# One store of a matmul kernel in 18 transfers: seven m tiles, 752 columns of the eighth, and its last 16 columns by 15, 14, down to 1, and 8 partitions

## Chip, cores and metric

One core of a Trainium2 chip. The metric is the device time of one execution in microseconds; a profile is one execution taken by the hardware profiler, and its span is shorter than that execution's time (208.6 and 210.41 for the kernel before). Runs were on several chips, so each kernel's time is compared with runs of the kernel before on the same chip. A profile of the kernel before was taken once, on the first chip; where a profile of an experiment is set against it, the chips can differ.

## The reference

```python
batch, m, k, n = 16, 512, 1024, 768
def reference(x, weight, sub_value):          # all float32
    return (np.matmul(x, weight) - sub_value).astype(np.float32)
```

Flattened, that is 8192 rows (64 m tiles of 128) by 1024 by 768; 87 MB go through the DMA engines: 62 MB read, 25 MB written.

## The kernel before

All transfers are issued from SyncE in the order of one list, `(kind, first m tile, number of m tiles)`. A transfer that is not ready holds up those after it (in the profile of before, SyncE stands still for up to 26.5 us before one of them).

```python
TRANSFERS = [
    ...                                             # loads of x ('x'), weight ('w') and sub_value ('s')
    ('o', 24, 8), ('o', 32, 8), ('s', 56, 8), ('o', 40, 8), ('o', 48, 8), ('o', 56, 5),
    ('o', 61, 2), ('o', 63, 1),                     # 'o': store
]
```

A store of eight tiles takes 24576 contiguous bytes from each of 128 partitions. Each issue waits for what it needs and adds 16 to a semaphore when it has landed:

```python
            if kind == "o":
                waits.append((counter["finish"], max(finish_at[t] for t in need)))
                ...
            sem, value = lane((kind, at))
            ...
            if kind == "o":
                here, there = there, here
            sp.add(lambda here=here, there=there: nc.sync.dma_start(out=here, in_=there), waits, (sem, 16))
```

sub_value and the result share one ring of 32 m tiles (`so_ring`): DVE subtracts in place. The tiles 40 to 47 are not loaded over again, so nothing waits for their store but the end of the kernel.

## Time and profile before

| | before |
|---|---|
| time, median of 2 | 210.31 us (210.26 to 210.35) |
| span of the profile | 208.6 us |
| last subtraction ends | 202.64 us |
| last store issued | 202.66 us |
| its first engine lands / its last engine lands | 204.86 / 207.29 us |
| SyncE instructions recorded | 68 |

The landings are read from the records of semaphore increments: each of the 38 transfers of the kernel before has 16 of them, 608 in all, one for each DMA engine that has finished its share, and the trace has the time of each. The prediction below shows the profile's lines and how they are read.

### The profile page before, as it was taken

The numbers are of one execution on the slowest core, as the hardware profiler recorded it, in microseconds if no ns is written. First come the engines' busy times: TensorE is split into PE (matmuls) and PEld (weight loads), VectorE is DVE, ScalarE is ACT, GpSimd is POOL, SyncE is SP. The second block draws the span as 40 slices with busy tenths as digits, with TensorE's granted clock in tenths as the row PEclk, the third lists the DMA queues.
The fourth block names the chain that finished last, engine by engine and source line by source line (L and its number), as shares of the span: only waits on it lengthen the run. The fifth ranks groups of instructions, "written<-read, shape, count | busy, mean of one in ns | idle before, by whom it ended". The sixth has DMA issues, their size and how long they took to land.

```text
span 208.6 us, 2612 instructions
## 1 busy us (share of the span) xinstructions
PE 195.2 (94%) x1234; PEld 75.5 (36%) x700; DVE 128.2 (61%) x224; ACT 109.0 (52%) x113; POOL 1.0 (0%) x7
## 2 busy tenths in 40 slices
PE   6999799969999999999999999999999999999960
PEld 0233243324434433443443443343344344334410
DVE  2323224975993795598399379469739938952330
ACT  3655759506673761944745576183564737507300
POOL 1000000000000000000000000000000000000000
PEclk9999999999999999999999999999999999999997
DMA  6999999999999999999999999999999999999993
GB/s 204 421 427 434 441 424 434 445 429 424 434 448 452 366 443 424 459 415 418 449 440 424 419 429 443 423 470 393 434 463 401 441 424 429 438 443 419 419 422 135
DMA packets 5476, 87.08 MB, mean 417 GB/s; under 512 B 608, under 2 KB 608, under 8 KB 1888
## 3 DMA queue, kind: packets, MB, share of 16 engines
q1 hardware_dynamic: 5472, 87.03, 97.9%
q8 instruction: 1, 0.02, 0.0%
q14 instruction: 3, 0.02, 0.0%
HBM read 61.87 MB, written 25.17 MB: 417 GB/s over the span
## 4 chain that ended last, share of the span: by engine, by line
PE 75%; DMA 13%; DVE 6%; SPq 3%; issue 1%; DVEq 0%
PE po_b L198 67%; DMA so_ring<-in_sub_value_dram 13%; PE pt_b L335 8%; DVE xtp_b L368 3%; DVE so_ring L417 2%; SPq L298 2%; SPq L262 1%; SPq L553 0%; DVEq L59 0%; SPq L138 0%
## 5 line engine op out<-in xcount | busy, mean ns | idle before, releaser
L198 PE MATMUL po_b<-w_sb,xt_b 128*128 128x384 f16 x704 | 126.0, 326 | 1.2 <-DVE w_sb L265 0.9
L417 DVE TENSOR_TENSOR so_ring<-po_b,so_ring 128x768 f32<-128x768 f32 x64 | 60.8, 957 | 59.3 <-PE po_b L198 39.9
L348 ACT COPY xt_b<-pt_b 128x1024 f16<-128x1024 f16 x44 | 44.5, 1012 | 65.3 <-PE pt_b L335 64.3
L368 DVE STREAM_TRANSPOSE xtp_b<-x16p_b 32x256 f32<-32x256 f32 x144 | 62.7, 435 | 2.3
L198 PE MATMUL po_b<-w_sb,xtp_b 128*128 128x384 f16 x320 | 61.3, 326 | 1.9 <-DVE xtp_b L368 1.7
L397 PEld LDWEIGHTS <-xt_b 128*128 128x128 f16 x352 | 34.4, 98 | 58.9 <-issue 55.6
L317 ACT CAST x_b<-x_ring 128x1024 f16<-128x1024 f32 x46 | 47.2, 1048 | 5.0 <-DMA x_ring<-in_x_dram 4.9
L335 PE MATMUL pt_b<-ident,x_b 128*128 128x128 f32 x184 | 47.5, 274 | 1.7 <-ACT x_b L317 1.7
L335 PEld LDWEIGHTS pt_b<-ident,x_b 128*128 128x128 f32 x184 | 25.4, 141 | 44.6 <-issue 36.8
L317 ACT CAST x16p_b<-x_ring 128x1024 f16<-128x1024 f32 x18 | 18.8, 1046 | 14.9 <-DMA x_ring<-in_x_dram 14.9
L397 PEld LDWEIGHTS <-xtp_b 128*128 128x128 f16 x160 | 15.7, 98 | 20.4 <-issue 18.3
L265 DVE CAST w_sb<-so_ring 128x768 f16<-128x768 f32 x8 | 4.1, 556 | 11.6 <-DMA so_ring<-in_weight_dram 11.6
L198 PE MATMUL po_b<-idle_x,idle_w 128*128 128x512 f16 x26 | 7.7, 448 | 1.7 <-POOL idle_x L178 1.7
L348 ACT COPY xtp_b<-pt_b 128x1024 f16<-128x1024 f16 x2 | 2.0, 1012 | 2.5 <-PE pt_b L335 2.5
L317 ACT ACT_TABLE_LOAD x1 | 1.3, 1283 | 0.9 <-SPq L138 0.9
L427 PEld LDWEIGHTS <-idle_w 128*128 128x128 f16 x4 | 0.4, 99 | 1.7 <-POOL idle_x L178 1.7
L187 DVE TENSOR_TENSOR ident<-along,across 32x32 f32<-32x32 f32 x4 | 0.7, 183 | 0.1
L179 DVE MEMSET ones<- 128x32 f32 x1 | 0.1, 85 | 1.0 <-SPq L138 1.0
L178 POOL MEMSET idle_x<- 128x512 f16 x1 | 0.5, 528 | 0.0
L499 ACT CAST stub<-ident 128x1 f16<-128x1 f32 x2 | 0.4, 194 | 0.0
L184 DVE STREAM_TRANSPOSE across<-along 128x32 f32<-128x32 f32 x1 | 0.2, 212 | 0.0
L476 POOL MEMSET mark<- 128x1 f32 x1 | 0.1, 98 | 23.7 <-ACT xtp_b L348 23.7
(7 smaller groups left out, 1.0 us busy)
## 6 DMA issues: line engine op xcount, KB each, us to landing
so_ring<-in_sub_value_dram SPq DMA_DIRECT2D x7, 3072.0 KB, 24.2
out_dram<-so_ring SPq DMA_DIRECT2D x7, 3072.0 KB, 26.6
x_ring<-in_x_dram SPq DMA_DIRECT2D x5, 4096.0 KB, 23.1
x_ring<-in_x_dram SPq DMA_DIRECT2D x2, 2048.0 KB, 27.2
so_ring<-in_weight_dram SPq DMA_DIRECT2D x4, 768.0 KB, 8.3
x_ring<-in_x_dram SPq DMA_DIRECT2D x1, 3072.0 KB, 28.8
x_ring<-in_x_dram SPq DMA_DIRECT2D x2, 1024.0 KB, 24.8
out_dram<-so_ring SPq DMA_DIRECT2D x1, 1920.0 KB, 10.2
```

Of the source, the lines that this page charges most:

```text
L178: pool.add(lambda: nc.gpsimd.memset(idle_x, 0.0), then=count("idle"))
L187: dve.add(lambda here=here: nc.vector.tensor_tensor(out=ident[here, here], in0=along[here], in1=across[here], op=mybir.AluOpType.is_equal, ...
L198: return nc.tensor.add_instruction(mybir.InstMatmult(name=nc.get_next_instruction_name(), engine=full.engine, ins=list(full.ins), outs=lis ...
L262: sp.add(lambda st=st, at=at: nc.sync.dma_start(out=st, in_=w_c[at]), then=(sem, 16))
L265: lambda at=at, r=r, st=st: nc.vector.tensor_copy(out=w_sb[:, at, r], in_=st[:, r]),
L298: sp.add(lambda here=here, there=there: nc.sync.dma_start(out=here, in_=there), waits, (sem, 16))
L317: act.add(lambda: nc.scalar.copy(out=to, in_=x_in), waits, count("cast"))
L335: pe.add(lambda: nc.tensor.transpose(words, from_, ident), waits, count("turn") if last else None)
L348: act.add(lambda: nc.scalar.copy(out=to, in_=pt_b[:, b]), waits, count("evac"))
L368: dve.add(lambda: nc.vector.transpose(xt[b * Q : (b + 1) * Q, :, a * Q : (a + 1) * Q], x16[a * Q : (a + 1) * Q, :, b * Q : (b + 1) * Q],), ...
L397: pe.add(lambda weights=weights: nc.tensor.ldweights(weights, tile_position=(0, 0)), [w for w in waits if w[0] in ready])
L417: dve.add(lambda: nc.vector.tensor_tensor(out=o, in0=po[:, :, :NS], in1=o, op=mybir.AluOpType.subtract), [landed["s", mi], (counter["mul"] ...
```

## The change

What the pattern is for, the code does not say; it names it `MARKED` and `PARTS`. The prediction assumes that a transfer of p partitions uses p DMA engines, and the same ones first each time, so that each of the first 15 small transfers uses one engine fewer than the one before it. The packet records have no engine numbers: engine 0, 1, ... are names, by the number of small transfers that an engine carries. The pattern either marks the engines in a trace or delays them by that number. The result of the kernel is the same.

```diff
+MARKED, PARTS = 40, tuple(range(15, 0, -1)) + (8,)
...
-            sp.add(lambda here=here, there=there: nc.sync.dma_start(out=here, in_=there), waits, (sem, 16))
+            if (kind, at) != ("o", MARKED):
+                sp.add(lambda here=here, there=there: nc.sync.dma_start(out=here, in_=there), waits, (sem, 16))
+                continue
+            edge, low = 752, 0
+            sp.add(lambda here=here, there=there: nc.sync.dma_start(out=here[:, : n - 1], in_=there[:, : n - 1]), waits, (sem, 16))
+            one = lane((kind, at, "edge"))
+            lanes_of = next(l for l in lanes if l["sem"] is one[0])
+            lanes_of["value"] += 16 * len(PARTS)
+            sp.add(lambda here=here, there=there: nc.sync.dma_start(
+                out=here[:, n - 1 :, :edge], in_=there[:, n - 1 :, :edge]
+            ), then=(one[0], 16))
+            for part in PARTS:
+                high = low + part
+                sp.add(lambda low=low, high=high, here=here, there=there: nc.sync.dma_start(
+                    out=here[low:high, n - 1 :, edge:], in_=there[low:high, n - 1 :, edge:]
+                ), then=(one[0], 16))
+                low = high
+            assert low == P
```

## The prediction

> **What bounds the kernel now.** I read the page's parts 1 and 2 first, then the table of windows, the chain of waits, the issues of the SyncE queue in order of time, and last the raw records behind them: one record per DMA packet (start, duration, size, but no engine number) and one per semaphore increment by a DMA.
>
> ```profile
> PE 195.2 (94%) x1234; PEld 75.5 (36%) x700; DVE 128.2 (61%) x224; ACT 109.0 (52%) x113; POOL 1.0 (0%) x7
> PE   6999799969999999999999999999999999999960
> ...
> DMA  6999999999999999999999999999999999999993
> GB/s 204 421 427 434 441 424 434 445 429 424 434 448 452 366 443 424 459 415 418 449 440 424 419 429 443 423 470 393 434 463 401 441 424 429 438 443 419 419 422 135
> ...
> q1 hardware_dynamic: 5472, 87.03, 97.9%
> ```
>
> Two things are full at once: TensorE (94%), and the 16 DMA engines (97.9% of the span, nine tenths or more in every slice but the first and the last). Which of them sets the end must be read at the end. The table of windows (columns: stretch, its length, busy us of each engine, granted clock, DMA share, GB/s):
>
> ```profile
> 180.00:190.00 10.00, 10.00 (x66) 3.79 (x36) 5.66 (x9) 4.23 (x7) 0.00 (x0) 1.00 1.00 430
> 190.00:200.00 10.00, 10.00 (x66) 3.94 (x37) 3.79 (x4) 3.98 (x4) 0.00 (x0) 1.00 1.00 430
> 200.00:204.00 4.00, 1.64 (x11) 0.39 (x4) 0.99 (x2) 0.00 (x0) 0.00 (x0) 1.00 0.95 402
> 204.00:206.00 2.00, 0.00 (x0) 0.00 (x0) 0.00 (x0) 0.00 (x0) 0.00 (x0) 1.00 0.54 220
> 206.00:208.60 2.60, 0.00 (x0) 0.00 (x0) 0.00 (x0) 0.00 (x0) 0.00 (x0) 0.51 0.04 15
> ```
>
> TensorE stops at 201.64, the last subtraction ends at 201.68 + 0.96 = 202.64, and the last store is issued at 202.66. The DMA engines are still full then, and run out one by one after 204: share 0.54, then 0.04. In the packet records every engine works without a gap up to its last packet; none waits for the last store. So the last stretch is bound by DMA bytes already queued, and the end is set by the engine that is furthest behind. The increments of the last store's semaphore show how far: the first engine lands at 204.86, twelve of them by 205.49, then 206.09, 206.48, 206.96 and 207.29. I call this last engine A: it is 2.43 us behind the first. The lags grew early: after landings with a spread of 0.7 us up to 28.7, A jumps to 1.80 at the landing of 32.3 and to 2.45 at 71.5, and then stays (2.43 at 112.7, 2.43 at 190.2). Between those jumps the engines keep the same pace. The runner-up is 0.3 us ahead of A.
>
> The chain of waits puts 75% on PE and 13% on the load of sub_value. Because it goes back from the last store through the last subtraction, it hides this DMA backlog; I don't read the bound of the last stretch from it.
>
> The stores concerned, from the timeline of the SyncE queue (start, duration):
>
> ```profile
> 170.88 0.34 SPq L298 DMA_DIRECT2D so_ring<-in_sub_value_dram  x1
> 171.27 0.62 SPq L298 DMA_DIRECT2D out_dram<-so_ring  x1
> ...
> 181.17 0.33 SPq L298 DMA_DIRECT2D out_dram<-so_ring  x1
> ...
> 194.32 0.33 SPq L298 DMA_DIRECT2D out_dram<-so_ring  x1
> ...
> 200.06 0.33 SPq L298 DMA_DIRECT2D out_dram<-so_ring  x1
> ```
>
> The store at 171.27 is the one that is split (m tiles 40 to 47). By its semaphore it lands at 190.24 to 192.67, since a store and the last sub_value load are queued before it. The next issue, at 181.17, waits for the subtraction of m tile 55.
>
> [...]The kernel before only has 128-partition transfers[...]: 38 transfers, 608 four-byte packets, 16 each. [...]the next data packet starts 4 to 6 ns after a semaphore packet does, though the increment is seen some 0.33 us later (206.96 and 207.29 for A).[...]
>
> **The change, part by part.** Bytes, waits, computing and the rest of the queue stay; 17 issues are added on SyncE. The order comparison shows the same rows on PE, DVE, ACT and POOL and 63 rows against 45 on SP (some rows merge repeats).
>
> (1) *SyncE's time.* One more issue costs 0.43 us (median of the ten stores). From 171.27: 0.62 + 17 x 0.48 (0.43 and the 0.05 gap seen between issues) = 8.8, so done at about 180.1. The next issue comes at 181.17. Free, with 1.1 us to spare; and even if an issue on fewer engines takes 0.7 us, the late store is at 184, while the engines have work queued up to about 190. Cost 0.
>
> (2) *The split of the rows into seven tiles and 752 columns.* Each engine gets 8 packets of 21504 B and 8 of 3008 B in place of 8 of 24576 B, and one semaphore packet more. Packets of 3072 B follow each other by about 117.5 ns, of 15360 B by about 569 ns: 36.7 ps per byte, and 4.6 ns for a packet. So 8 x 4.6 + 6 (semaphore packet) = 0.04 us on every engine.
>
> (3) *The 16 small ones.* [...]Engine 0 gets 16 of them (15 and the last 8), engine 7 gets 8 + 1 = 9, engine 8 gets 7, engine 14 one, engine 15 none; 128 in all, 8 on average. By the fit of (2), a small one is 64 x 0.0367 + 4.6 + 6 = 13 ns; with the recorded durations (8 ns for the 40-byte packets, 9 ns for a semaphore packet) it is about 19. [...]Engine 0: 16 x 19 = 0.30 us, at 60 ns 1.0 us. An average engine: 0.15 us, or 0.5.
>
> (4) *What of it counts.* All of this lies inside the backlog, and no buffer waits for this store (no sub_value load comes after the one at 170.88). What A gets is paid in full at the end. An engine ahead of A pays only what exceeds its lead: 12 of 16 engines lead by at least 1.8 us and can't become last below 110 ns for a small one. The numbers of A and the runner-up aren't in the records. If A is engine 15: +0.04. If it is engine 0: +0.34, up to +1.1 us. On average over the places, +0.2 at 19 ns, +0.5 at 60. I take +0.3 us.
>
> Sum: 210.31 + 0.3 = 210.6 us. The intent looks like moving a little work by engine number, or marking the engines: transfers that each leave out one engine more. But it takes no work off a late engine: 64 B of 8 rows are 512 B, 0.02 us.
>
> **The rivals.** (R1) *A small semaphore write stalls its engine.* If 16 stalls of 0.33 us come in a row, engine 0 is 5.3 us late; minus its lead, the end comes 3 to 5 us later, 213.3 to 215.6. Against it: 4 to 6 ns after every semaphore packet before. For it: they were never nearer together than 0.94 us per engine. 6%. (R2) *The number of transfers that may be outstanding is limited.* At the start, the 14th, 15th and 16th issue take 0.98, 1.65 and 2.13 us instead of 0.43. About 10 transfers, or about 90 packets per engine, were outstanding then. If packets are the limit: at the end of the small issues engine 0 has about 24 + 9 + 32 = 65, no block. If transfers are: SyncE blocks after some six small ones until the queue drains at 185 to 192, the next store is issued late, at about 193 to 196, and the engines run dry for 2 to 5 us: 212.5 to 215.5. 10%. (R3) *An instruction fetch falls elsewhere.* Four packets of 8 or 16 KB of other queues lie in the span (at 30.9, 50.4, 87.5, 146.0), and after each of them one engine's lag jumps by 0.5 to 1.1 us. SyncE's stream grows from 68 to 85 instructions; should that bring one more fetch or another engine, the end moves by up to 1 us either way. 10%. (R4) *A gain*: only by R3, or if the end is not set by A; under 0.3 us.
>
> **Range and chances.** The plain sum gives 210.35 to 210.65, dear small writes up to 211.4; R3 adds up to 1 us; R1 and R2 make the upper tail. The two runs of before differ by 0.09. Prediction 210.6, eight times in ten within 210.2 to 211.8. Two per cent are 4.2 us: slower needs R1 or R2 in full, 5%; faster has no source, 1%.
>
> **What would show each step.** (1) 55 issues on SyncE; the small ones at some 0.48 us each; the next store still at about 181.2. An issue of over 1 us, or a later store, speaks for R2. (2) and (3): 128 packets of 64 B at about 10 ns; small transfers landing with k increments by DMA, 15 down to 1 and 8; the time between the landings of the split store and the next one, 7.27 us before, grows by 0.04 us on the engine without small ones and by up to 0.3 on the one with 16. A gap of 0.3 us after each small one is R1. (4) The last store's landing at 207.3 to 207.7, TensorE and DVE unchanged. The prediction is wrong if the DMA share falls below 0.9 between 185 and 200, or if the spread of the last landing exceeds 3.5 us.

## The result, and the profile after

212.69 us (212.67 to 212.70, 2 runs) against 210.31: ratio 1.0109, 95% interval 1.0085 to 1.0133. A ratio here is the mean time of one kernel's fast runs over that of the other's fast runs of the same rounds, so it is not quite the ratio of the medians quoted; the differences in us given for the experiments are these ratios times the time before. The kernel is 2.4 us slower, and outside the range of 210.2 to 211.8.

The page of the changed kernel (parts 1 to 3):

```profile
PE 195.7 (93%) x1234; PEld 75.5 (36%) x700; DVE 128.1 (61%) x224; ACT 108.9 (52%) x113; POOL 1.0 (0%) x7
...
DMA  5999999999999999999999999999999999999991
GB/s 197 421 427 432 435 423 443 444 427 430 424 462 429 390 443 424 416 466 395 438 466 404 443 438 406 472 416 407 477 416 420 448 420 415 422 414 395 407 398 68
DMA packets 5877, 87.08 MB, mean 413 GB/s; under 512 B 880, under 2 KB 880, under 8 KB 2288
```

The engines do the same work. The packets below 512 B went from 608 to 880: 128 small ones and 144 semaphore packets (16 for the 752 columns, 128 for the small transfers). The table of windows of the changed kernel, and of the one before for the first two stretches:

```profile
190.00:192.00 2.00, 2.00 (x16) 0.95 (x9) 0.96 (x1) 1.47 (x2) 0.00 (x0) 1.00 1.27 400
192.00:194.00 2.00, 2.00 (x15) 0.90 (x9) 0.59 (x1) 0.92 (x2) 0.00 (x0) 1.00 0.95 363
...
200.00:204.00 4.00, 1.71 (x11) 0.39 (x4) 1.07 (x2) 0.00 (x0) 0.00 (x0) 1.00 0.94 402
204.00:206.00 2.00, 0.00 (x0) 0.00 (x0) 0.00 (x0) 0.00 (x0) 0.00 (x0) 1.00 0.77 316
206.00:208.00 2.00, 0.00 (x0) 0.00 (x0) 0.00 (x0) 0.00 (x0) 0.00 (x0) 0.73 0.28 115
208.00:211.00 3.00, 0.00 (x0) 0.00 (x0) 0.00 (x0) 0.00 (x0) 0.00 (x0) 0.50 0.03 11
```

```profile
190.00:192.00 2.00, 2.00 (x15) 0.94 (x9) 0.96 (x1) 1.54 (x2) 0.00 (x0) 1.00 1.03 442
192.00:194.00 2.00, 2.00 (x15) 0.91 (x8) 0.67 (x1) 0.92 (x2) 0.00 (x0) 1.00 1.11 479
```

This is the main reading. TensorE is as busy as before, and works until 201.71 (before: 201.64). Between 190 and 194, where the small transfers are worked off, the DMA engines stay busy by the share, but carry 400 and 363 GB/s instead of 442 and 479: over 4 us, 2 x (442 + 479 - 400 - 363) = 316 KB less. The engines are occupied without moving bytes. (A share over 1 is possible because packets are counted by the time at which they start.)

SyncE's queue issued the small ones without trouble:

```profile
171.26 0.70 SPq L304 DMA_DIRECT2D out_dram<-so_ring  x1
172.00 0.71 SPq L308 DMA_DIRECT2D out_dram<-so_ring  x1
172.76 7.44 SPq L313 DMA_DIRECT2D out_dram<-so_ring  x16
181.24 21.82 SPq L301 DMA_DIRECT2D out_dram<-so_ring  x4
```

Sixteen issues in 7.44 us, and the next store at 181.24 against 181.17. The time was lost on the DMA engines. The packet records (times in ns from the span's start) of one engine, whose small ones can be told apart because the engine is late:

```
start   end     took  bytes
192488  192497     9      4     semaphore packet of the 752 columns
192494  192505    11     64     1st small one; 13 small ones and 13 semaphore packets, 13 ns from one to the next
...
192657  192666     9      4     13th semaphore packet
192662  194422  1760  24576     next store: 912 ns otherwise
194419  195919  1500  24576
```

The small ones are passed in 13 x 13 = 169 ns, as predicted. The two packets behind them take 1760 and 1500 ns instead of 912: 1.44 us more. The number of small ones in a row names the engine, if the same engines come first in every transfer: 13 small ones is engine 3, the only one that is then in the 12 transfers of 15 down to 4 and in the last of 8. The extra time of the packets behind, for the engines told with certainty: 2 or 3 small ones 0; 5 (engine 10) 0; 6 (engine 9) 0.18; 12 (engine 4) 1.63; 13 (engine 3) 1.44; 15 (engine 1) 1.65 us. The other engines, told apart by the distance between two packets, fit between: 7 about 0.34, 9 to 11 about 1.0 to 1.4, 16 (engine 0) 1.92. In sum 12.2 us over 16 engines, 0.76 each; at 430 GB/s that is 328 KB, the 316 KB missing in the windows.

The increments of the last store's semaphore give the end: first engine 205.20 (before 204.86), last engine 209.09 (before 207.29). In the change, engine 3 is last. It was 2.38 us behind the first engine when the seven tiles landed, 0.17 us of small packets and 1.44 us of stretching make 3.99; measured 3.89. Engine 10, which was last before the small ones, 3.03 us behind the first, had only five of them and is passed.

After the last landing there are 1.8 us to the end of the span, against 1.3 before. The profile's view of the last lines of SyncE, before and after (columns: operation, duration min/median/max in ns, first and last start in us):

```profile
L526 SPq EVENT_SEMAPHORE  x1: 17/17/17, 207.5 to 207.5; - x1
L526 SPq DRAIN  x1: 7/7/7, 207.6 to 207.6; - x1
```

```profile
L545 SPq EVENT_SEMAPHORE  x1: 17/17/17, 209.3 to 209.3; - x1
L545 SPq DRAIN  x1: 124/124/124, 209.7 to 209.7; - x1
```

The gap between the two instructions was 68 ns and is 430 ns, and the drain itself takes 124 instead of 7: 0.48 us, with nothing waited for that the profile shows.

So the spans' difference of 2.3 us is 1.8 us of later landing and 0.5 us behind it. Of the 1.8, some 0.16 is not the change's: the load of x tiles 56 to 63 already begins to land at 161.29 instead of 161.13, before anything is different.

### The profile page after: what moved, and what is told of

It is laid out like the page before. It is cut to its first block, busy times and chain, and to the rows that moved or that the text cites.

```text
span 210.9 us, 2630 instructions
## 1 busy us (share of the span) xinstructions
PE 195.7 (93%) x1234; PEld 75.5 (36%) x700; DVE 128.1 (61%) x224; ACT 108.9 (52%) x113; POOL 1.0 (0%) x7
## 4 chain that ended last, share of the span: by engine, by line
PE 74%; DMA 13%; DVE 5%; SPq 3%; issue 1%; DVEq 0%
PE po_b L200 67%; DMA so_ring<-in_sub_value_dram 13%; PE pt_b L354 7%; DVE xtp_b L387 3%; DVE so_ring L436 2%; SPq L301 2%; SPq L264 1%; SPq L572 0%; DVEq L61 0%; SPq L140 0%
```

## The experiments

Theory after the result, from the semaphore packets and the stretched ones behind them: each engine of a transfer confirms it with a semaphore increment (128 semaphore packets for the 16 small ones); a few in a row are free (5: 0), but many hold back the engine's next data packets (13: 1.44 us). I call this a completion. Rivals: writes as small as 64 bytes are dear in themselves; the number of transfers or SyncE's issues cost; all completions share one place (theory S) instead of being slow on each engine (theory P). The runs were made in four groups, each on one chip, with five rounds. Beside e1 to e4 the kernel before was 210.65 us (210.36 to 211.18), beside e5 to e8 210.62, beside e9 to e12 210.68, beside e13 and e14 210.58. "Extra" below is the sum of what the 24576-byte packets behind the small ones took above 912 ns on one engine.

### e1: two transfers

```diff
-MARKED, PARTS = 40, tuple(range(15, 0, -1)) + (8,)
+MARKED, PARTS = 40, ()
...
-            edge, low = 752, 0
+            edge, low = n_cols, 0        # n_cols = N = 768
...
```

> The store of tiles 40 to 47 in two transfers, seven tiles and the whole eighth; none is small. Both theories (stalled completions; dear 64-byte writes) expect the 0.04 us of the extra packets and nothing else: 210.3 to 210.5 us, a spread of the last landing of 2.3 to 2.6 us as before. If splitting the store is itself dear, 210.8 or more.

210.70 us, ratio 1.0003 (0.9990 to 1.0017); the last landing has a spread of 2.55 us, no packet is stretched by over 0.06. No cost of splitting a store can be seen; the interval allows up to 0.36 us.

### e2: one small transfer

```diff
+MARKED, PARTS = 40, (128,)
```

> Three transfers: seven tiles, 752 columns, and the last 16 columns of all 128 partitions at once: the same 128 packets of 64 bytes, 8 on each engine, but one completion per engine in place of up to 16. Theory (each completion of a store keeps its engine's writes back, and many in a row add up): 210.3 to 210.6 us, and the packets after the small ones keep their 912 ns. Rival (the 64-byte write itself is dear, 0.12 us each): 8 x 0.12 on every engine, 211.2 to 211.5 us and stretched packets after them.

211.04 us, ratio 1.0014 (1.0002 to 1.0026), 0.3 us. The same 128 packets of 64 bytes, 8 on each engine: they start 7 ns apart, and behind them nothing is stretched by over 0.1 us. That is 9 GB/s on one engine, against 27 for a packet of 24576 bytes in 912 ns. The windows of this kernel:

```profile
190.00:192.00 2.00, 2.00 (x15) 0.91 (x8) 0.96 (x1) 1.36 (x2) 0.00 (x0) 1.00 1.13 461
192.00:194.00 2.00, 2.00 (x15) 0.86 (x8) 0.49 (x1) 0.92 (x2) 0.00 (x0) 1.00 0.98 418
```

Sum 879, against 921 before and 763 in the change. These small writes are not what is dear. The time is nonetheless above what was expected: in this profile two late engines lose 0.75 and 0.68 us at 182 us, before the small ones reach them. That is taken up at e13.

### e3: 512 bytes wide

```diff
-            edge, low = 752, 0
+            edge, low = 640, 0
```

> The 18 transfers of the change with the same partitions, but the small ones 128 columns (512 bytes) wide in place of 16. Theory (completions): like the change, 212.5 to 213.0 us (engine 3 also carries 5 x 512 bytes more than its share, 0.1 us), packets after the small ones stretched by 0.5 to 1.9 us on the engines with 9 to 16 of them. Rival [...]: no stretching, about 210.5 us, or 211.0 with the late end of SyncE that the trace of the change shows.

212.27 us, ratio 1.0073 (1.0056 to 1.0090), 1.5 us, and in the profile 10.5 us of extra in sum (the change: 12.2), up to 1.7 on one engine. At eight times the width the extra is nearly the same: it goes with the number of transfers in a row, not with their width. The size was expected a little larger (212.5 at least).

### e4: only the instructions

The kernel before, and behind the issue of the store:

```diff
+            if (kind, at) == ("o", 40):
+                filler = tc.alloc_semaphore("filler")
+                for i in range(17):
+                    sp.add(lambda: nc.sync.sem_inc(filler, 1))
```

> The store whole, as before, and 17 instructions that only count up an unused semaphore behind it on SyncE, so that its stream is as long as the changed one. Theory (the 0.43 us by which SyncE's second-last drain starts late after the last landing comes from the longer stream): the last landing as before, the end 0.3 to 0.5 us later, 210.6 to 210.8 us, and in the trace a gap of about 0.4 us between SyncE's last semaphore increment and the drain after it. If the late drain belongs to the transfers: 210.3 us, a gap below 0.1 us.

211.08 us, ratio 1.0021 (1.0009 to 1.0033), 0.4 us, with the last landing at 207.16 as before. The gap is there, 418 ns, but one instruction later, between the drain and the no-operation behind it (start of the last one 207.9):

```profile
L530 SPq NOP  x2: 13/15/17, 206.8 to 207.9; - x2
L530 SPq EVENT_SEMAPHORE  x1: 17/17/17, 207.4 to 207.4; - x1
L530 SPq DRAIN  x1: 7/7/7, 207.4 to 207.4; - x1
```

Counting SyncE's recorded instructions explains it. In the change the gap lies between the 79th and the 80th; here, with one instruction less, also between the 79th and the 80th. So it is in all kernels with 85 to 87 of them: e3, e5 and e7 (430, 430 and 429 ns, before the drain), e9 (429, behind it), e12 (415, before the semaphore increment). Kernels with up to 78 have none. With 94 (e10) and 102 (e6) the gap lies ahead of the wait for the last landing. In e6 (416 ns, from 202.97) it is hidden behind that wait. In e10 (423 ns, up to 208.67) it is not: SyncE reaches the wait at 209.03, 0.29 us after the last landing, and the end comes 1.68 us after the landing, against 1.30 in the kernel before. The gap belongs to a place in the stream, whatever stands there, not to the transfers. A fetch of instructions goes with it. The pages of the kernel before and of the change count the packets of a queue that the trace names "instruction":

```profile
q14 instruction: 3, 0.02, 0.0%
```

```profile
q14 instruction: 4, 0.03, 0.0%
```

Every kernel with the gap has this one packet of 8 KB more. It starts 0.6 to 0.7 us after the gap has ended (in the change at 210.38; in e6 2.5 us after it). In e8 and e11, with 78 and 75 instructions, it comes behind the end of the span; the kernels with up to 73 have none. So the gap and that packet come with the length of SyncE's stream; what SyncE does in the gap, no record shows.

### e5: the change again

> The changed kernel again, to have it beside the others on one chip: 1.5 to 2.5 us over before. In the trace, the packets behind the small ones stretched by 0.5 to 1.9 us on the engines with 9 to 16 small transfers, not at all on those with up to 5; SyncE's late drain of 0.4 us.

212.50 us, ratio 1.0079 (1.0064 to 1.0094), 1.7 us. The extra: engine 1 1.74, engine 3 1.46, engine 4 1.60, engine 10 0.05 us. The same four engines are late as in the first profile of the change, and the same one comes last (lag 3.77). The change costs 1.7 us here and 2.3 on the first chip, where it had only two runs; the intervals just overlap.

### e6: four engines

```diff
+MARKED, PARTS = 40, (4,) * 32
```

> 32 small transfers of 4 partitions: again 128 packets and 128 completions, but 32 on each of engines 0 to 3 and none on the others. Theory P (each engine takes about 0.2 us for each completion, by itself): the stretching on these four grows from 1.9 us (16 completions) to about 4.6, the end 4.5 to 6 us over before. Theory S (all engines share one place that takes about 25 ns per completion, 128 of them in 3.2 us): the stretching stays at 1.5 to 2.2 us, the end 2.3 to 3.3 us over before (engine 3 was late by 2.1 us to begin with).

215.48 us, ratio 1.0220 (1.0206 to 1.0235), 4.6 us. Exactly four engines have the stretched packets:

```
start   end     took  bytes
190976  195636  4660  24576        195632  197094  1462  24576
191094  195618  4524  24576        195614  197087  1473  24576
191650  196168  4518  24576        196165  197580  1415  24576
193180  197754  4574  24576        197750  199241  1491  24576
```

That is 4.1 to 4.3 us of extra each. The small transfers' last increments come 0.18 us apart (193.88, 194.06, 194.24, 194.42, 194.61, ...), with all four engines adding one each time. Theory S, with its 1.5 to 2.2 us of stretching, falls; an engine works off its own completions, one in about 0.18 us. The windows at the end show the engines that are left over, a quarter of the 16:

```profile
206.00:208.00 2.00, 0.00 (x0) 0.00 (x0) 0.00 (x0) 0.00 (x0) 0.00 (x0) 0.50 0.28 114
208.00:210.00 2.00, 0.00 (x0) 0.00 (x0) 0.00 (x0) 0.00 (x0) 0.00 (x0) 0.50 0.25 103
210.00:213.70 3.70, 0.00 (x0) 0.00 (x0) 0.00 (x0) 0.00 (x0) 0.00 (x0) 0.50 0.04 16
```

Here SyncE was also held up: its 32 small issues took 17.0 us, one of them 2.26, and the next store went out at 189.93. The engines without small ones ran dry for it (at 190.6 to 190.8 the records have a packet under way on 8 of 16 engines): ten of them land that store within 0.12 us of one another, from 198.50 on (the change: 197.86). It does not set this end, since engine 3 has work all along.

### e7: four at a time

The same 16 small transfers, four of them behind each of the stores of tiles 40, 48, 56 and 61:

```diff
...
+                for small in later[:4] if kind == "o" else []:
+                    sp.add(small, then=(one_sem[0], 16))
+                if kind == "o":
+                    del later[:4]
...                                        # the small transfers are put into the list `later`
```

> The same 16 small transfers, but in groups of four behind the last four stores but one, several us apart, so that no engine ever has more than four in a row. Both theories of the completions: an engine with up to 5 in a row lost nothing in the change, so nothing is stretched; what is left is SyncE's late drain and the 0.1 to 0.2 us of packets: 0.4 to 0.7 us over before. If the number of small transfers counts and not their being in a row: as the change, 1.5 to 2.5.

211.32 us, ratio 1.0029 (1.0013 to 1.0046), 0.6 us, and no packet behind them is stretched by over 0.14 us (one of 15360 bytes; those of 24576 bytes by at most 0.08). The drain is late as in the change:

```profile
L554 SPq EVENT_SEMAPHORE  x1: 17/17/17, 208.0 to 208.0; - x1
L554 SPq DRAIN  x1: 124/124/124, 208.4 to 208.4; - x1
```

The end comes 1.87 us after the last landing, 0.57 more than before, which is nearly all of the 0.6. So the completions cost by standing in a row; the same number, spread out, costs nothing that can be seen but SyncE's late end.

### e8: all engines

```diff
+MARKED, PARTS = 40, (16,) * 8
```

> 8 small transfers of 16 partitions: 128 packets and completions again, 8 on every engine. Theory P: 8 in a row cost an engine 0.5 to 0.7 us, on all engines, 0.7 to 1.3 us over before with 0.15 us of packets and perhaps SyncE's late drain. Theory S: 128 completions at one place take 3.2 us whoever sends them, so all 16 engines are stretched by 1.3 to 2 us, 1.5 to 2.6 us over before.

211.50 us, ratio 1.0050 (1.0030 to 1.0069), 1.0 us. All 16 engines are stretched, by 0.40 to 0.93 us, 0.59 on average: theory P (0.5 to 0.7), not S (1.3 to 2). With e2 this parts the completions from the packets: the same 8 packets of 64 bytes on each engine, but 8 completions in place of one. The increments of the small transfers come 0.22 to 0.29 us apart, somewhat slower than with four engines, so something is shared after all, but it does not set the size.

### e9: loads

The kernel before, and behind the store the same 16 shapes as loads from x into an unused tile `spare`:

```diff
...
+                    sp.add(lambda low=low, high=high: nc.sync.dma_start(
+                        out=spare[low:high], in_=x_flat[low:high, :16]
+                    ), then=(one[0], 16))
```

> The store whole as before, and behind it the 16 small transfers as loads: the same partitions, 64 bytes each, from x into an unused tile. If it is the write into HBM whose confirmation takes an engine some 0.18 us for each completion, [...]nothing is stretched: 0.4 to 0.7 us over before, SyncE's late drain and the packets. If each completion costs that whatever it confirms: as the change, 1.5 to 2.4 us over, with packets stretched by 0.5 to 1.9 us.

212.43 us, ratio 1.0081 (1.0060 to 1.0103), 1.7 us, up to 1.97 us of extra, 12.7 in sum. A load's completions cost as much as a store's (12.7 against 12.2 us in sum), so the confirmation of the small writes into HBM is not the cause.

### e10: a semaphore each

```diff
-            lanes_of["value"] += 16 * len(PARTS)
...
             for part in PARTS:
                 high = low + part
+                one = lane((kind, at, low))
```

> The change, with a semaphore of its own for each of the 17 later transfers. If the increments wait for one another because they go to one semaphore: completions closer together than 0.18 us per engine and little stretching, 0.4 to 0.9 us over before. If the engine works off its completions one by one wherever they go: as the change, 1.5 to 2.4 us over, engine with 16 of them stretched by about 1.9 us.

212.20 us, ratio 1.0078 (1.0057 to 1.0100), 1.6 us, up to 1.86 us of extra, 11.7 in sum. The common semaphore is not the cause either.

### e11: five in a row on every engine

```diff
+MARKED, PARTS = 40, (16,) * 4 + (64,)
```

> The small part in five transfers (four of 16 partitions, one of 64): five completions in a row on every engine, behind that of the 752 columns. In the change an engine with 5 lost nothing. If that number is a real allowance: no packet stretched by over 0.1 us behind the small ones, 0.0 to 0.4 us over before. If every completion costs 0.15 us from the first: 5 x 0.15 on all engines, 0.8 to 1.1 us over.

211.43 us, ratio 1.0031 (1.0017 to 1.0045), 0.65 us, between the two expectations. Ten engines have at most 0.04 us of extra, five have 0.05 to 0.21, one 0.31. So five are free when few engines have as many, as in the change, and not quite when all do. There is no sharp allowance.

### e12: engine 0 alone

```diff
+MARKED, PARTS = 40, (1,) * 16 + (112,)
```

> 16 small transfers of one partition, all on engine 0, and one of 112 partitions: 17 completions in a row on engine 0, one on each other. Engine 0 is stretched by about 2.0 us and gets 0.2 us of packets; if it is one of the engines that were about 2 us ahead of the last, it comes out level with the last or up to 0.4 us behind it. With SyncE's late drain: 0.4 to 0.9 us over before. If the stretching of one engine slows all of them, or the number of transfers is what costs: 1.5 us or more.

211.23 us, ratio 1.0023 (1.0008 to 1.0037), 0.5 us. One engine is stretched, by 2.03 us, the others by at most 0.09. The last landing has lags of ..., 0.65, 1.71, 2.10, 2.40 and 2.75 us: the last engine is the one that was last before the small ones (2.76). An engine that is 2 us ahead can lose 2 us without becoming last. Of the 0.5 us, 0.3 is SyncE's gap: the end comes 1.62 us after the last landing, against 1.30.

### e13: four large transfers, and e14: an early store

These two ask for what was still unexplained. In the profiles of all kernels with small transfers, one to three packets at 182 to 184 us are stretched by 0.1 to 0.75 us on late engines, while the small ones still wait in the queue; in e1 and e4 none is, before one by 0.14.

```diff
-    ... ('s', 56, 8), ('o', 40, 8), ('o', 48, 8), ...
+    ... ('s', 56, 8), ('o', 40, 2), ('o', 42, 2), ('o', 44, 2), ('o', 46, 2), ('o', 48, 8), ...     # e13
-    ... ('x', 16, 2), ('x', 18, 6), ('s', 16, 8), ('x', 24, 8), ('o', 0, 8), ...
+    ... ('x', 16, 2), ('o', 0, 1), ('x', 18, 6), ('s', 16, 8), ('x', 24, 8), ('o', 1, 7), ...        # e14
```

> The store in four transfers of two tiles each, none small: three completions more, each 1.8 us from the next. If the stretched packets at 182 to 184 come from the number of transfers and packets waiting in the queue, they appear here too, by 0.2 us or more on one of the late engines, and the time is 0.2 to 0.6 us over before. If they belong to small transfers: none over 0.1 us there, 0.0 to 0.2 us over before (24 packets more per engine are 0.11 us).

> The kernel before with m tile 0 stored by itself some 20 us earlier, so that the first write to the output does not meet the loads of x tile 24. If the stretched packets at 68 to 70 us (7 us in sum over the engines of the kernel before, 1.1 us on the last one) belong to the first store, they move to about 45 us and most likely stay as large: time as before within 0.3 us. If they come from the long store behind the long load, they shrink with it, and the end comes up to 0.7 us earlier.

e13: 211.13 us, ratio 1.0022 (1.0008 to 1.0036), 0.5 us, but no packet at 182 to 184 us is stretched, and the last engine's lag is 2.70; it was 2.67 already at 161 us, before this kernel differs from the one before. The profile speaks for the small ones, the time for the number of transfers: undecided. e14: 210.84 us, ratio 1.0008 (0.9994 to 1.0022). The stretched packets at 68 to 70 us, which all other profiles have, are gone, but the last engine's lag jumps by 0.75 us at the early store instead, from 1.86 to 2.61. The end is not sooner. It was the one attempt at a kernel faster than both; there is none.

## Why the prediction was wrong

**What bounds the kernel: right.** DMA bytes that are queued, and the engine furthest behind, set the end. TensorE, DVE and the issue of the last store (202.74 against 202.66) hardly moved, and the time follows the last landing in every profile, up to SyncE's late end. e12 shows the rule on leads at work.

**(1) SyncE's time: right.** The small issues took 0.25 to 1.07 us, 0.46 on average with the gaps, and the next store was issued at 181.24. One issue took over 1 us, which was to be a sign of R2, but the next store was not late.

**(2) The split: not contradicted.** e1 is 0.03% slower, 0.06 us, where 0.04 were expected; its interval of -0.2 to 0.36 us is too wide to show so small a cost.

**(3) The small ones: this step failed.** "By the fit of (2), a small one is 64 x 0.0367 + 4.6 + 6 = 13 ns." The packets do pass in 13 ns, and the allowance of up to 60 ns for one, which no trace had shown, was needless (e2, e3). The counts by engine came as assumed: one engine was stretched by transfers of 1 partition (e12), four by transfers of 4 (e6), all by transfers of 16 (e8). Which engines of the 16 these are no record shows. The missing term is the completion. Engine 0's 16 small ones were put at 0.30 us, 1.0 at the worst; measured are 0.21 us of packets and 1.92 us of stretching behind them. Engine 3's 13: 0.17 and 1.44. e3, e6, e7, e9 and e10 show that completions in a row on one engine do it, whatever their size, direction or semaphore.

**(4) What counts: right as a rule, wrong in its sizes.** "12 of 16 engines lead by at least 1.8 us and can't become last below 110 ns for a small one." The small ones came to (1.92 + 0.21) / 16 = 133 ns on engine 0, but that engine did not become last; the runner-up did, engine 3, for which 0.3 us of lead was foreseen (0.65 in this profile: 3.03 against 2.38). Of the prediction's own signs of being wrong, one came true: the spread of the last landing is 3.89, over 3.5. The other, a DMA share below 0.9, did not; the share is no measure of bytes here.

**R1 was the right rival with 6%.** It expected a semaphore write to stall its engine in a row of many, 0.33 us each, 213.3 to 215.6 us. It was turned down because the packet behind a semaphore packet starts 4 to 6 ns after it. That observation holds in the change too, and proves nothing: the stall is not a gap between packets but a longer packet, and it needs many completions in a row, which the trace of the kernel before, with 0.94 us between them at least, could not show. They follow one another by 0.18 us, not 0.33, and the first few are nearly free.

**R2 did not happen in the change** (with 32 small transfers, e6, its signs came: SyncE was held up and engines ran dry). **R3 happened in another form:** the longer SyncE stream cost 0.42 to 0.48 us (e4, the change) by a gap of SyncE itself behind the last landing. It did bring one more fetch, but at 210.38, when the last store had landed and there was no DMA work left to delay. The place was not foreseen.

The sum as it should have been, on the first chip's pair of profiles: engine 3's lag of 2.38 with 0.17 and 1.44 us, less the 2.43 by which the last engine lagged before, make 1.56 (1.46 measured); the first engine is 0.34 later, of which 0.16 was there before the change acts; SyncE's gap is 0.48. With the measured 1.46 that is 2.3 us, the difference of the spans.

**What stays open.** Why completions in a row hold back data, and what the allowance of about five is. Each small transfer has exactly one completion on each of its engines, so no run parts the semaphore increment from anything else that an engine may do once for each transfer; the increments that come 0.18 us apart while the packets pass in 13 ns (e6) speak for the increment. Why e2, e11 and e13 are 0.3 to 0.65 us slower than before although little is stretched behind their small transfers, and what stretches packets at 182 to 184 us.

## What to carry to other kernels

In this kernel, whose DMA engines are busy until the queue ends (share 1.00 from 180 to 200 us before, 1.00 and 1.03 in the change), many small transfers in a row cost their engines 0.15 to 0.23 us each from about the sixth on (e6: 4.2 us for the 27 beyond the fifth; engine 4 in the change: 1.63 us for 7), although the packets pass in 13 ns. What helped was to spread them between long transfers (e7: 24576-byte packets stretched by at most 0.08 us), or to make one transfer of them (e2: at most 0.1). A transfer of few partitions loaded as few engines (e12: one; e6: four), the same ones each time, and what it cost the kernel depended on whether one of these was among the engines that were last anyway (e12: 2.03 us of stretching, 0.5 us of time; e6: 4.1 to 4.3 and 4.6). A busy share near 1 did not show that DMA engines move bytes (192 to 194 us: share 0.95 with 363 GB/s in the change, 1.11 with 479 before): compare GB/s in windows.
